# Hybrid MLA and S5 encoder layer: all of x projected ahead of the state tables, and one refinement per latent tile

## The chip, the cores and the metric

The kernel runs on one core of a Trainium2 chip. The metric is the device time of one execution in microseconds; it was measured in three runs, and the median counts. The profile is one execution taken by the hardware profiler.

## What is computed

One inference step of an encoder layer over 1152 tokens of width 1024: 1024 of a new stream, and 8 running streams with 16 new tokens each. One projection of the normalised tokens feeds an attention part (384 numbers of a query latent, 256 of a key and value latent, 32 of a rotary key) and a state space part, S5 (512 channels in 32 groups of 16, each group driving 64 complex states). Behind both come an output projection and a gated feed-forward network with a causal convolution, which is most of the work. Cut to what the change touches (`lb` is the exponential of `a * dt`, `bb` the input matrix scaled by it):

```python
hin = _rmsnorm(x, g_mix_norm) @ w_in
q_lat, c_kv_lat, k_pe, u = split(hin, [384, 256, 32, 512])
c_q  = _rmsnorm(q_lat, g_q_a)              # mean square over 384
c_kv = _rmsnorm(c_kv_lat, g_kv_a)          # mean square over 256, an output
k_pe = _rope(k_pe)                         # an output
s = scan(s[t] = lb * s[t-1] + bb @ u[t])   # per channel group, complex
y = Re(C s) + D * u
o_b = gelu(y) * sigmoid(gelu(y) @ w_glu + b)
h = x + concat(o_a, o_b) @ w_out
out = h + ConvFFN(_rmsnorm(h, g_ffn_norm))
```

`_rmsnorm(v, g)` is `v * rsqrt(mean(v*v) + 1e-6) * g`.

## The kernel before, in words

All matrix products of weight and activation are made of three TensorE passes over a high and a low part of each factor (`mm3`, line 137). The tokens lie in three blocks of 384 columns, block 2 ending with the running streams; a block has three latent tiles of 128 tokens, nine in all (tiles 0 to 8).

Phase A (`phase_a`) is the part around the change. Its pieces:

- `load_x(b, k)` loads a 128-row slice of block b of x (eight make the block), splits it, and sums its squares; `load_w` loads and splits a slice of the projection's weights: `wuh`, `wul` for the S5 channels, `wnh`, `wnl` for the latents.
- `stats(b)` makes the tokens' scale (`ssx`, `rb` on TensorE), and `upart(b)` projects the block to S5 channels: four output blocks `up` of 128x384, 24 matmuls each, scaled to `us` and stored to `u_dram`. With `kouter` it takes the slices in the order in which they come, all four outputs at a time; without, one output after the other.
- `natpart(i)` makes latent tile i: two outputs `nat` (128x384 and 128x288, 24 matmuls each), the Square and the refinement `rsqrt_act` of each (a square root on ScalarE, then a reciprocal and one Newton step on VectorE), and its stores to `cq_dram`, `ckv_dram` and the output.
- `tables()` makes the S5 tables. VectorE and GpSimd form `epre` in 8 pieces, TensorE transposes them (`ep`, four to a piece, line 322), ScalarE evicts to `es` and SyncE stores to `e_dram`; then `fo` in 8 pieces, stored to `f_dram`, and the products `kp` (line 343, four to a piece), evicted to `kts` and stored to `kt_dram`.
- `s5_early` loads `Et` from `e_dram`; `s5_load_u` loads `U` from `u_dram`, in 8 loads of 16 partitions each, in pieces of 144 numbers; both lie in space that the tables' tiles held. `s5_states` multiplies them (`pst`, line 420) and evicts the two parts to `RI`.

Behind that `s5_scan` runs on VectorE and GpSimd (products of complex numbers, lines 373 to 407), and `s5_out` makes the outputs (`py`, line 530) from the states `SP` and a table `Ft`. The sample attention (`b8_q`, `phase_b`: keys `pk`, scores `pS`, rotated keys `pRK`, sums of keys `ssk`) lies beside and behind the scan.

The program is written in one order, but a scheduler orders every engine's list from it, by its own estimates of time; each engine, and SyncE's queue of loads and stores, then works its list strictly in order. Block 1 of x lies in the buffer that block 2 held, so it can be split only when tiles 8, 7 and 6 are done; block 0 has a buffer of its own.

Of the kernel before, what the change touches and what calls it, by code (L numbers as in the profile page):

```python
# [13 lines left out]
AF = mybir.ActivationFunctionType  # L14
# [60 lines left out]
def build(tc, t):  # L75
    nc = tc.nc
# [3 lines left out]
    with root:  # L80
# [69 lines left out]
        def rsqrt_act(pool, y, x, scale, tag):  # L150
            v = pool.tile(list(x.shape), F32, tag=tag + "v", name="rsv")
            w = pool.tile(list(x.shape), F32, tag=tag + "w", name="rsw")
            ts(v, x, scale, EPS, ALU.mult, ALU.add)
            nc.scalar.activation(out=w, in_=x, func=AF.Sqrt, scale=scale, bias=epsc)
            nc.vector.reciprocal(out=y, in_=w)
            stt(w, y, -0.5, y, ALU.mult, ALU.mult)
            mul(w, w, v)
            stt(y, w, 1.5, y, ALU.add, ALU.mult)
# [194 lines left out]
        def s5_early():  # L353
            es = s5t["es"] = root.enter_context(ExitStack())
            s5a = es.enter_context(tc.tile_pool(name="s5a", bufs=1, side="right", reuse_waits="tile"))
            s5t["pool"] = s5a
            Et = s5t["Et"] = s5a.tile([P, G, P], F32, tag="ES", name="Et", padded_shape=[P, G, NCH])
            s5t["U"] = s5a.tile([P, G, NCH], F32, name="U")
            load(Et, e_dram)
# [259 lines left out]
        def phase_a():  # L619
            st = ExitStack()  # L620
            with st:
                a = st.enter_context(tc.tile_pool(name="a", bufs=1))
                sg = st.enter_context(tc.tile_pool(name="asg", bufs=2))
                xb = None
                wnh = a.tile([P, 8, NATW], F32R, name="wnh")
# [3 lines left out]
                def load_x(b, k):  # L629
                    if k == 0:  # L630
                        xp = xb if b == 0 else a
                        xhl[b] = (xp.tile([P, 8, TB], F32R, tag="xhi", name="xhi"),
                                  xp.tile([P, 8, TB], F32R, tag="xlo", name="xlo"))
                    s = al["p"].tile([P, TB], F32, tag="xs", name="xs", bufs=XB[0])
                    load(s, t["xT"][k * P:(k + 1) * P, b * TB:(b + 1) * TB])
                    split(xhl[b][0][:, k], xhl[b][1][:, k], s, gmix[:, k:k + 1])
                    if k == 0:
                        accx[b] = al["p"].tile([P, TB], F32, tag="accx", name="accx", bufs=1)
                        nc.scalar.activation(out=accx[b], in_=s, func=AF.Square)
                    else:  # L640
                        q = al["p"].tile([P, TB], F32, tag="sqx", name="sqx")
                        nc.scalar.activation(out=q, in_=s, func=AF.Square)
                        add(accx[b], accx[b], q, nc.gpsimd if b == 0 else None)

                def load_w(k, hi, lo, c0):
                    n = hi.shape[2]
                    w = al["p"].tile([P, NATW], F32, tag="ws", name="ws", bufs=XB[1])
                    load(w[:, 0:n], t["w_in"][k * P:(k + 1) * P, c0:c0 + n])
                    split(hi[:, k], lo[:, k], w[:, 0:n], eng=nc.gpsimd if k % 2 else None)
# [8 lines left out]
                def stats(b):  # L658
                    c = slice(3 * b, 3 * b + 3)
                    p_ = psum("t", [P, 3], "ssx")  # L660
                    for i in range(3):
                        nc.tensor.matmul(p_[:, i:i + 1], lhsT=accx[b][:, i * P:(i + 1) * P], rhs=ones[:, 0:1], start=True, stop=True)
                    rsqrt_act(al["p"], rx[:, c], p_, 1.0 / DM, "rx")
                    p_ = psum("t", [P, TB], "rb")
                    for i in range(3):
                        rr = al["p"].tile([P, P], F32, tag="rr", name="rr", bufs=3)
                        ts(rr, ones, rx[:, 3 * b + i:3 * b + i + 1], None, ALU.mult)
                        nc.tensor.transpose(p_[:, i * P:(i + 1) * P], rr, ident)
                    Rb[b] = al["p"].tile([P, TB], F32, tag="Rb", name="Rb")
                    acopy(Rb[b], p_)  # L670

                def upart(b, kouter=False):
                    xh, xl = xhl[b]
                    nck = TB // LC
                    pu = {}

                    def step(cb_, k):
                        c0 = cb_ * P
                        if k == 0:
                            pu[cb_] = psum("u", [P, TB], "up")  # L680
                        mm3(pu[cb_], [((wuh[:, k, c0:c0 + P], wul[:, k, c0:c0 + P]), (xh[:, k], xl[:, k]))], first=k == 0, last=k == 7)

                    if kouter:
                        for k in range(8):
                            for cb_ in range(4):
                                step(cb_, k)
                    else:
                        for cb_ in range(4):
                            for k in range(8):
                                step(cb_, k)  # L690
                    for cb_ in range(4):
                        us = al["p"].tile([P, TB], F32, tag="us", name="us").rearrange("p (j c) -> p j c", j=LC)
                        mul(us.rearrange("p j c -> p c j"), pu[cb_].rearrange("p (c j) -> p c j", j=LC),
                            Rb[b].rearrange("p (c j) -> p c j", j=LC))
                        store(u_dram[cb_ * P:(cb_ + 1) * P, :, b * nck:(b + 1) * nck], us)

                def natpart(i):
                    b = i // 3
                    xh, xl = xhl[b]
                    tsl = slice((i % 3) * P, (i % 3 + 1) * P)  # L700
                    n = sg.tile([P, NATW], F32, tag="nat", name="nat")
                    sq = sg.tile([P, 2], F32, tag="sq2", name="sq2")
                    rq = sg.tile([P, 2], F32, tag="rq2", name="rq2")
                    jk = sg.tile([P, QL], BF16, tag="jk2", name="jk2", bufs=1)
                    for z, (c0, c1) in enumerate(((0, QL), (QL, NATW))):
                        p_ = psum("s", [P, c1 - c0], "nat")
                        mm3(p_, [((xh[:, k, tsl], xl[:, k, tsl]), (wnh[:, k, c0:c1], wnl[:, k, c0:c1])) for k in range(8)])
                        acopy(n[:, c0:c1], p_, rx[:, i:i + 1])
                        w = (QL, KL)[z]
                        nc.scalar.activation(out=jk[:, 0:w], in_=n[:, c0:c0 + w], func=AF.Square, accum_out=sq[:, z:z + 1])  # L710
                        rsqrt_act(sg, rq[:, z:z + 1], sq[:, z:z + 1], 1.0 / w, f"rq{z}")
                    cq, ck = n[:, 0:QL], n[:, QL:QL + KL]
                    ts(cq, cq, rq[:, 0:1], None, ALU.mult)
                    store(cq_dram[i * P:(i + 1) * P], cq)
                    stt(ck, ck, rq[:, 1:2], gkv, ALU.mult, ALU.mult)
                    store(ckv_dram[i * P:(i + 1) * P], ck)
                    store(t["ckv"][i * P:(i + 1) * P], ck)
                    x2 = n[:, QL + KL:NATW].rearrange("p (a d) -> p a d", a=2)
                    m1 = sg.tile([P, 2, 16], F32, tag="m1", name="m1")
                    m2 = sg.tile([P, 2, 16], F32, tag="m2", name="m2")  # L720
                    mul(m1, x2, cosb[:, i:i + 1].to_broadcast([P, 2, 16]), nc.gpsimd)
                    mul(m2, x2, sinb[:, i:i + 1].to_broadcast([P, 2, 16]), nc.gpsimd)
                    sub(kpe[:, i, 0:16], m1[:, 0], m2[:, 1], nc.gpsimd)
                    add(kpe[:, i, 16:32], m1[:, 1], m2[:, 0], nc.gpsimd)
# [11 lines left out]
                load(ident, t["ident"])  # L736
                stats(2)
                for k in range(8):
                    load_x(0, k)
                late_consts()  # L740
                load(gkv, t["g_kv"])
                stats(0)
                for k in range(8):
                    load_w(k, wnh, wnl, 0)
                upart(2, True)
                upart(0, True)
                tables()
                s5_early()
                for i in (8, 7, 6):
                    natpart(i)  # L750
                for k in range(8):
                    load_x(1, k)
                stats(1)
                upart(1)
                ust.close()
                s5_open()
                s5_load_u()
                s5_states()
# [966 lines left out]
```

## Time and profile before

| what | us |
|---|---|
| median of the three runs | 1581.94 |
| lowest and highest | 1581.4, 1583.57 |
| span of the profiled execution | 1582.0 |
| TensorE busy | 1497.2 (95%) |
| VectorE busy | 1119.5 (71%) |
| ScalarE busy | 683.8 (43%) |
| GpSimd busy | 320.6 (20%) |

Busy time is the time in which an engine worked on an instruction; what is missing to the span it waited. The page gives the span for the profiled execution and no other time of it. A share over the whole span says little of a stage: the first 400 us hold phase A, the scan and the start of the attention, the other 1180 us the attention's rest and the feed-forward network.

### The profile page before, as it was taken

How to read it: one execution, taken by the hardware profiler on the slowest of the kernel's cores; microseconds unless marked ns; L12 is line 12 of the kernel's file. 1: busy time of each engine (PE TensorE's matmuls, PEld its weight loads, DVE VectorE, ACT ScalarE, POOL GpSimd, SP SyncE). 2: the span in 40 equal slices, each digit the busy share in tenths (PEclk: the TensorE clock that was granted, in tenths of full speed). 3: DMA queues.
4: the chain of work that ended last, by engine and by line, in shares of the span. 5: the costliest groups of instructions: out<-in, count | busy, mean ns of one | idle time of the engine just before them, and what ended most of it. 6: DMA issues, size and time to landing. Idle time of an engine off the chain costs nothing.

```text
span 1582.0 us, 24076 instructions
## 1 busy us (share of the span) xinstructions
PE 1497.2 (95%) x8861; PEld 1427.5 (90%) x8861; DVE 1119.5 (71%) x2376; ACT 683.8 (43%) x1323; POOL 320.6 (20%) x616
## 2 busy tenths in 40 slices
PE   7896857999999999999999999999999999999998
PEld 6876745877888898999999999999999999999998
DVE  8983799485777676367676766776766777777766
ACT  6442346666666676434433333333333333333321
POOL 3550466130444222112100000000100000000000
PEclk9998867999999999999999999999999999999999
DMA  7449343463321222451021111111111111111103
GB/s 203 122 144 161 114 154 57 111 186 97 97 69 48 78 65 65 151 165 52 1 84 37 41 41 41 50 45 40 41 41 41 46 49 51 44 41 40 41 1 130
DMA packets 101205, 122.00 MB, mean 77 GB/s; under 512 B 39240, under 2 KB 81416, under 8 KB 100624
## 3 DMA queue, kind: packets, MB, share of 16 engines
q1 hardware_dynamic: 100960, 120.44, 27.1%
q8 instruction: 69, 1.13, 0.3%
q14 instruction: 48, 0.39, 0.1%
q0 software_dynamic: 128, 0.03, 0.0%
HBM read 93.79 MB, written 26.65 MB: 76 GB/s over the span
## 4 chain that ended last, share of the span: by engine, by line
PE 80%; DVE 11%; DMA 4%; ACT 2%; issue 1%; SPq 1%; POOL 0%; DVEq 0%; ACTq 0%
PE pu L137 35%; PE pd L137 16%; PE pw L137 6%; DVE w L104 3%; PE pk L137 3%; PE pst L1247 2%; PE pg L137 1%; PE pq L137 1%; PE psm L1214 1%; PE pst L1248 1%; PE po L1260 1%; PE po L1262 1%; PE pst L1249 1%; PE pS L137 1%; PE po L1261 1%
## 5 line engine op out<-in xcount | busy, mean ns | idle before, releaser
L104 DVE TENSOR_TENSOR hT<-hT,pd 128x384 f32<-128x384 f32 x528 | 288.2, 551 | 211.7 <-PE pd L137 211.6
L137 PE MATMUL pu<-hnh,wl 128*128 128x384 f32 x1056 | 353.9, 335 | 0.0
L137 PE MATMUL pu<-hnl,wh 128*128 128x384 f32 x1056 | 353.9, 335 | 0.0
L137 PE MATMUL pu<-hnh,wh 128*128 128x384 f32 x1056 | 353.6, 335 | 0.0
L137 PE MATMUL pd<-act,wh 128*128 128x384 f32 x1056 | 348.0, 336 | 0.5 <-DVE hT L104 0.4
L1532 ACT ACTIVATE c<-pu,cvh 128x384 f32<-128x384 f32 x132 | 88.7, 672 | 302.1 <-PE pu L137 302.0
L137 PEld LDWEIGHTS pd<-act,wh 128*128 128x128 f32 x1056 | 197.7, 188 | 2.4 <-DVE hT L104 2.3
L137 PEld LDWEIGHTS pu<-hnh,wh 128*128 128x128 f32 x1056 | 198.2, 188 | 0.0
L137 PEld LDWEIGHTS pu<-hnl,wh 128*128 128x128 f32 x1056 | 198.2, 188 | 0.0
L137 PEld LDWEIGHTS pu<-hnh,wl 128*128 128x128 f32 x1056 | 198.0, 187 | 0.0
L122 DVE SCALAR_TENSOR_TENSOR c<-u,cvh,c 128x256 f32<-128x256 f32 (+1 forms) x352 | 171.1, 516 | 26.8 <-ACT u L101 13.8
L137 PE MATMUL pd<-act,wl 128*128 128x384 f32 x528 | 178.3, 338 | 0.0
L101 ACT ACTIVATE act<-c 128x384 fp32r<-128x384 f32 x66 | 34.7, 526 | 158.8 <-DVE c L104 158.8
L137 PEld LDWEIGHTS pd<-act,wl 128*128 128x128 f32 x528 | 99.2, 188 | 0.0
L1538 POOL COPY u<-u 128x2 f32<-128x2 f32 x88 | 20.0, 228 | 379.1 <-DVE c L104 172.1
L104 DVE TENSOR_TENSOR wl<-ws,wh 128x1024 fp32r<-128x1024 f32 x74 | 91.0, 1234 | 6.0 <-ACT wh L101 6.0
L101 ACT ACTIVATE wh<-ws 128x1024 fp32r<-128x1024 f32 x74 | 78.0, 1057 | 11.7 <-PE pw L137 6.5
L1550 POOL COPY cvo<-u 128x2 f32<-128x2 f32 x44 | 8.1, 184 | 353.9 <-ACT u L101 353.9
L1218 DVE TENSOR_REDUCE mx<-psm 128x1 f32<-128x512 f32 (+2 forms) x96 | 52.3, 550 | 29.8 <-PE psm L1216 15.0
L1554 ACT ACTIVATE c<-c 128x384 f32<-128x384 f32 x66 | 34.7, 526 | 75.1 <-DVE c L122 75.0
L101 ACT ACTIVATE u<-pu 128x384 f32<-128x384 f32 (+2 forms) x176 | 66.2, 404 | 0.0
L137 PE MATMUL pw<-oh,wh 128*128 128x384 f32 x192 | 64.9, 339 | 0.0
(468 smaller groups left out, 3174.6 us busy)
## 6 DMA issues: line engine op xcount, KB each, us to landing
ws<-in_w_up SPq DMA_DIRECT2D x44, 512.0 KB, 3.7
ws<-in_w_down SPq DMA_DIRECT2D x22, 512.0 KB, 3.6
xs<-in_xT SPq DMA_DIRECT2D x24, 192.0 KB, 3.5
os<-o_dram SPq DMA_DIRECT2D x24, 192.0 KB, 2.7
hT<-in_xT SPq DMA_DIRECT2D x24, 192.0 KB, 4.3
out_yT<-hT SPq DMA_DIRECT2D x24, 192.0 KB, 2.1
cf<-in_cT SPq DMA_DIRECT2D x8, 512.0 KB, 4.7
cn<-in_cn SPq DMA_DIRECT2D x8, 512.0 KB, 7.1
```

What stands on the lines that cost most here:

```text
L101: nc.scalar.activation(out=out, in_=in_, func=AF.Copy, scale=scale)
L104: (eng or nc.vector).tensor_tensor(out=out, in0=a, in1=b, op=op)
L122: nc.vector.scalar_tensor_tensor(out=out, in0=a, scalar=s, in1=b, op0=op0, op1=op1)
L137: nc.tensor.matmul(out, lhsT=w, rhs=x, start=first and i == 0, stop=last and i == n - 1)
L1214: nc.tensor.matmul(p_[:, u, 0:n], lhsT=lh, rhs=kT[jj][0][0:QD, 4 * g + h, 0:n], start=True, stop=not dg)
L1218: nc.vector.tensor_reduce(out=mx[:, h, z, hb:hb + 1], in_=p_.rearrange("p a k -> p (a k)")[:, 0:tot], axis=AX.X, op=ALU.max)
L1247: nc.tensor.matmul(o_, lhsT=kh[:, 4 * g + h, ks], rhs=qh[:, h, qs_], start=True, stop=False)
L1248: nc.tensor.matmul(o_, lhsT=kl[:, 4 * g + h, ks], rhs=qh[0:QD, h, qs_], start=False, stop=False)
L1249: nc.tensor.matmul(o_, lhsT=kh[0:QD, 4 * g + h, ks], rhs=ql[:, h, qs_], start=False, stop=not dg)
L1532: nc.scalar.activation(out=c, in_=p_, func=AF.Identity, scale=w[2], bias=w[3])
L1538: nc.gpsimd.tensor_copy(out=u[:, 0:2], in_=halo[i, gv][:, TB:TB + 2])
L1554: nc.scalar.activation(out=g_, in_=g_, func=AF.Silu)
```

## The change

In the program's order, latent weights are loaded ahead of block 0 of x; block 2's channels and its three latent tiles come first; then block 0 and block 1 are loaded and their channels projected, block 1's slice by slice as well; then come the tables and the load of `Et`, and the S5 states. The other six latent tiles stay where they were in the program, behind the S5 states. In `natpart` the Square scales its input, so that its sum is a mean, and one refinement on 128x2 takes the place of two on 128x1.

```diff
--- before.py
+++ after.py
@@ -707,8 +707,8 @@
                         mm3(p_, [((xh[:, k, tsl], xl[:, k, tsl]), (wnh[:, k, c0:c1], wnl[:, k, c0:c1])) for k in range(8)])
                         acopy(n[:, c0:c1], p_, rx[:, i:i + 1])
                         w = (QL, KL)[z]
-                        nc.scalar.activation(out=jk[:, 0:w], in_=n[:, c0:c0 + w], func=AF.Square, accum_out=sq[:, z:z + 1])
-                        rsqrt_act(sg, rq[:, z:z + 1], sq[:, z:z + 1], 1.0 / w, f"rq{z}")
+                        nc.scalar.activation(out=jk[:, 0:w], in_=n[:, c0:c0 + w], func=AF.Square, scale=w ** -0.5, accum_out=sq[:, z:z + 1])
+                    rsqrt_act(sg, rq, sq, 1.0, "rq")
                     cq, ck = n[:, 0:QL], n[:, QL:QL + KL]
                     ts(cq, cq, rq[:, 0:1], None, ALU.mult)
                     store(cq_dram[i * P:(i + 1) * P], cq)
@@ -736,23 +736,23 @@
                 load(ident, t["ident"])
                 stats(2)
                 for k in range(8):
-                    load_x(0, k)
+                    load_w(k, wnh, wnl, 0)
                 late_consts()
                 load(gkv, t["g_kv"])
-                stats(0)
-                for k in range(8):
-                    load_w(k, wnh, wnl, 0)
                 upart(2, True)
-                upart(0, True)
-                tables()
-                s5_early()
                 for i in (8, 7, 6):
                     natpart(i)
                 for k in range(8):
+                    load_x(0, k)
+                stats(0)
+                upart(0, True)
+                for k in range(8):
                     load_x(1, k)
                 stats(1)
-                upart(1)
+                upart(1, True)
                 ust.close()
+                tables()
+                s5_early()
                 s5_open()
                 s5_load_u()
                 s5_states()
```

What the scheduler makes of it: TensorE, at the first table transposes (`ep`). `nat` is a latent tile's output, `up` one of S5 channels. Before:

```order
L137 MATMUL nat<-wnl,xhi 128x384
L137 MATMUL nat<-wnh,xhi 128x384
L322 MATMUL ep<-ident,epre 128x128 [waits DVE_49,PE_49]
L322 MATMUL ep<-ident,epre 128x128 x3
L137 MATMUL nat<-wnh,xlo 128x384
```

Now:

```order
L137 MATMUL up<-xhi,wuh 128x384
L137 MATMUL up<-xhi,wul 128x384
L137 MATMUL up<-xlo,wuh 128x384
L322 MATMUL ep<-ident,epre 128x128 [waits Activation_49]
L322 MATMUL ep<-ident,epre 128x128 x3
L137 MATMUL nat<-wnl,xhi 128x288
```

The first `ep` stood at row 251 of TensorE's list, among latent matmuls; it stands at row 453 now, behind the last projection of block 1, and 288-column latent matmuls follow it.

SyncE's queue, at the loads of `Et` and `U`. Before:

```order
L98 DMA kt_dram<-kts 16x512 [waits DMAHW0_49,DVE_49]
L95 DMA Et<-e_dram 128x32x128 [waits DMAHW1_49,PE_49,Pool_49]
L95 DMA h_1420<-in_h 128x256 [waits DMAHW2_49]
L98 DMA u_dram<-us 1024x1x48 [waits DMAHW3_49,DVE_49]
L98 DMA u_dram<-us 1024x1x48 [waits DMAHW4_49,DVE_49]
L98 DMA cq_dram<-nat 128x384 [waits DMAHW5_49,DVE_49]
L98 DMA u_dram<-us 1024x1x48 [waits DMAHW6_49,DVE_49]
L98 DMA u_dram<-us 1024x1x48 [waits DMAHW7_49,DVE_49]
L98 DMA ckv_dram<-nat 128x256 [waits DMAHW0_49,DVE_49,Activation_49]
L98 DMA out_ckv<-nat 128x256 [waits DMAHW1_49]
L95 DMA U<-u_dram 16x32x144 [waits DMAHW6_49,DMAHW4_49,DMAHW7_49,DMAHW3_49,DMAHW2_49]
L95 DMA U<-u_dram 16x32x144 x2
```

Now:

```order
L98 DMA kt_dram<-kts 16x512 [waits DMAHW3_49,DVE_49]
L95 DMA Et<-e_dram 128x32x128 [waits DMAHW4_49,PE_49,Pool_49]
L95 DMA U<-u_dram 16x32x144 [waits DMAHW6_49,DMAHW5_49,DMAHW3_49]
L95 DMA U<-u_dram 16x32x144
L95 DMA U<-u_dram 16x32x144 [waits DMAHW7_49]
L95 DMA U<-u_dram 16x32x144 [waits DMAHW0_49]
L95 DMA U<-u_dram 16x32x144 [waits DMAHW1_49]
L95 DMA U<-u_dram 16x32x144 [waits DMAHW2_49]
```

Four stores of `u_dram`, three of a latent tile and a load of `h` stood between `Et` and `U`, and the eight loads of `U` now follow `Et` at once.

TensorE, at the S5 states (`pst`). `tq` belongs to the sample attention. Before:

```order
L572 MATMUL tq<-ident,cq_1763 128x128 [waits DMAHW2_49]
L420 MATMUL pst<-U,Et 128x144 [waits DVE_49]
L420 MATMUL pst<-U,Et 128x144 x2
L137 MATMUL nat<-wnl,xhi 128x384
L137 MATMUL nat<-wnh,xhi 128x384
L137 MATMUL nat<-wnh,xlo 128x384
L137 MATMUL nat<-wnl,xhi 128x384
L137 MATMUL nat<-wnh,xhi 128x288
L137 MATMUL nat<-wnh,xlo 128x288
L420 MATMUL pst<-U,Et 128x144 [waits DVE_49]
L137 MATMUL nat<-wnl,xhi 128x288
L420 MATMUL pst<-U,Et 128x144 [waits DVE_49]
```

Now:

```order
L137 MATMUL nat<-wnh,xhi 128x288
L137 MATMUL nat<-wnh,xlo 128x288
L137 MATMUL nat<-wnl,xhi 128x288
L420 MATMUL pst<-U,Et 128x144 [waits DMAHW4_49,DMAHW5_49,DMAHW3_49,DMAHW6_49,DMAHW2_49,DMAHW7_49,DMAHW1_49,DMAHW0_49]
L420 MATMUL pst<-U,Et 128x144 x11
L420 MATMUL pst<-U,Et 128x144 [waits DVE_49]
```

Latent matmuls stood between the `pst` and behind them; now the last latent matmul of the kernel comes directly ahead of the first `pst`, and all 32 `pst` follow one another.

## Rows read from the trace of the kernel before

**Rows 1.** The page: span, busy time of TensorE.

```profile
span 1582.0 us, 24076 instructions
...
PE 1497.2 (95%) x8861; PEld 1427.5 (90%) x8861; DVE 1119.5 (71%) x2376; ACT 683.8 (43%) x1323; POOL 320.6 (20%) x616
```

**Rows 2.** By stage: window, its length, engines' busy us (instructions), clock, DMA share.

```profile
core 0: us, PE busy (x) PEld busy (x) DVE busy (x) ACT busy (x) POOL busy (x), PEclk, DMA share, GB/s
...
117.30:158.30 41.00, 25.89 (x167) 25.55 (x166) 15.85 (x92) 9.26 (x28) 2.79 (x12) 0.85 0.99 157
158.30:174.80 16.50, 16.50 (x108) 16.47 (x109) 8.20 (x20) 8.68 (x22) 0.37 (x1) 0.86 0.82 255
174.80:275.00 100.20, 67.53 (x281) 53.39 (x281) 97.17 (x245) 47.47 (x107) 68.80 (x105) 0.74 0.32 85
275.00:306.00 31.00, 31.00 (x215) 28.84 (x214) 16.08 (x46) 22.06 (x39) 6.31 (x9) 1.00 0.32 85
...
401.60:1582.00 1180.40, 1172.27 (x7110) 1140.83 (x7108) 820.68 (x1602) 480.01 (x914) 165.01 (x413) 1.00 0.19 58
```

**Rows 3.** Timeline, TensorE: start, us, instruction, [idle before, releaser].

```profile
58.38 0.44 PE L137 MATMUL nat<-wnl,xhi 128*128 128x384 f32 x1 [0.64 <-POOL wnl L104]
...
66.44 0.63 PE L322 MATMUL ep<-ident,epre 128*128 128x128 f32 x4 [1.49 <-DVE epre L104]
...
114.91 1.05 PE L343 MATMUL kp<-fo,bb 128*16 128x128 f32 x8
...
158.27 5.49 PE L420 MATMUL pst<-U,Et 128*128 128x144 f32 x24 [15.11 <-DMA krf<-in_kropeT]
...
274.92 0.41 PE L530 MATMUL py<-SP,Ft 128*128 128x144 f32 x2
...
305.91 0.41 PE L530 MATMUL py<-SP,Ft 128*128 128x144 f32 x2
```

**Rows 4.** Timeline, SyncE's queue, from the last table store to U.

```profile
116.85 0.30 SPq L98 DMA_DIRECT2D kt_dram<-kts  x1
117.26 0.60 SPq L95 DMA_DIRECT2D Et<-e_dram  x1
...
135.04 10.12 SPq L95 DMA_DIRECT2D U<-u_dram  x8
```

**Rows 5.** Chain of waits, 110 to 180 us: start, length, what.

```profile
142.67 15.40 DMA U<-u_dram
...
174.80 1.56 DVE w L104 x3
```

**Rows 6.** VectorE's groups up to 265 us: form, count | busy us, mean ns.

```profile
L104 DVE TENSOR_TENSOR rsw<-rsw,rsv 128x1 f32<-128x1 f32 x18 | 6.5, 362 | 0.3
...
L122 DVE SCALAR_TENSOR_TENSOR rsw<-rq 128x1 f32<-128x1 f32 x18 | 6.0, 332 | 0.3
...
L122 DVE SCALAR_TENSOR_TENSOR rq<-rsw,rq 128x1 f32<-128x1 f32 x18 | 4.4, 245 | 0.3
```

**Rows 7.** Timeline, TensorE: two 384-column matmuls in a dense stretch.

```profile
118.05 0.33 PE L137 MATMUL up<-xhi,wul 128*128 128x384 f32 x1
118.22 0.33 PE L137 MATMUL up<-xlo,wuh 128*128 128x384 f32 x1
```

**Rows 8.** By stage, columns as rows 2: table work, dense work, Et, U.

```profile
60.00:120.00 60.00, 51.96 (x314) 45.88 (x313) 53.56 (x116) 22.59 (x53) 38.11 (x36) 0.94 0.47 136
120.00:140.00 20.00, 20.00 (x132) 19.95 (x131) 11.27 (x64) 7.57 (x21) 1.93 (x8) 1.00 0.86 189
118.70:127.00 8.30, 8.30 (x57) 8.26 (x56) 5.58 (x38) 2.18 (x6) 0.00 (x0) 1.00 0.99 272
136.00:157.00 21.00, 7.16 (x47) 6.84 (x45) 3.30 (x15) 2.90 (x10) 0.87 (x4) 0.74 1.20 120
```

## The prediction, made before the changed kernel was run

> **What bounds the kernel now.** I read the page first: TensorE is busy for 1497.2 of 1582.0 us, so the end is set by TensorE wherever nothing holds it up [rows 1]. Then the span cut into stages, to see where it is held up. From 401.6 us on it is busy for 1172.27 of 1180.40 us at full clock; nothing there is touched, and that stretch can only start earlier or later. The stages ahead are where a change can act: 117.3 to 158.3 (25.89 busy of 41.00), and 174.8 to 275, where VectorE is busy for 97.17 of 100.20 and TensorE for 67.53 [rows 2].
>
> Then the timeline and the chain, to see what hands the stages on. The first transpose of the state tables (`ep`) starts at 66.44, the last product (`kp`) at 114.91 [rows 3]; SyncE, one queue in order, issues the last `kt_dram` store at 116.85 and the load of Et behind it at 117.26, and the loads of U only from 135.04 [rows 4], since the last `u_dram` stores (block 1) come out late. TensorE then stands idle for 15.11 us until `pst` starts at 158.27 [rows 3]. That row names another load as the releaser; the chain says what it waited for: U [rows 5]. Behind `pst` the S5 scan starts on VectorE (174.80), and the output products `py` run from 274.92 to 305.91 [rows 3, 5]. So to first order the path is: table end, Et and U, `pst`, scan on VectorE, `py`, then a TensorE queue with hardly a gap. It gives the price rule: a microsecond on the path ahead of the scan is a microsecond at the end, except for TensorE work that leaves the stretch behind the scan.
>
> A run here varies by some 2 us (1581.4 to 1583.57), so 0.2%, 3.2 us, is what can be told from no change. The profiled span of 1582.0 is the median of the runs (1581.94) within 0.1 us, and the sum is made against it.
>
> **Part 1: one refinement per tile.** Per tile one Sqrt on ScalarE and five VectorE operations of 128x1 go, 9 and 45 in all; the Square's scale replaces a multiply that the refinement did. The rows give, for 18 each, 6.5 + 6.0 + 4.4 us [rows 6]; half of them is 8.5 us, and the two short ones (reciprocal, scale and add) bring it to some 10 us of VectorE. In 117.3 to 158.3 VectorE is busy for 15.85 of 41 us [rows 2], so most of it lies where VectorE waits anyway, and I give it nothing there. In the scan stage the changed order has no latent tile left at all, which frees more, but it has also pulled sample attention (sums of keys, their refinements) in there: counted from instructions by their rows, VectorE's list from the first scan operation to the second final state goes from 94.5 to 97.7 us. That is +3, not a gain.
>
> **Part 2: where the tables end.** The changed TensorE order puts 114 projections of S5 channels and 72 + 50 latent matmuls ahead of the first `ep`, counted from 58.4 us, up to which the two orders do the same. Dense pitch of a 384-column matmul is 0.17 us [rows 7]; a 288-column one has three quarters of that, 0.13. So 186 x 0.172 + 50 x 0.131 = 38.5, and 1.5 for the small ones: first `ep` at 99, not 66.4. Behind it, up to the last `kp`, stand 32 transposes, 66 + 70 latent matmuls and 32 `kp`: a group of four `ep` takes 0.63 us and one of four `kp` (eight passes) 1.05 [rows 3], so 5.0 + 20.5 + 8.4 = 34. Dense, the last `kp` is at 133.5. But in 60 to 120, the same kind of mix, TensorE was busy for 51.96 of 60 us (87%), against 20.00 of 20 in 120 to 140 where no table work runs [rows 8]. With 87% in both pieces it is at 145. I take 140: the first piece has little table work between its matmuls and should run nearly dense, and the second is loaded with transfers (by the queue's list some 10 MB between 104 and 142 us, 260 GB/s, where 60 to 120 moved 136). Et is then issued 2.35 us behind, as before (114.91 to 117.26): **142, 24.5 later than before**.
>
> The cover lost: in the kernel before, 24 projections and five latent tiles stood behind the tables and filled the wait for Et and U. Now three tiles are left to fill it, 54 x 0.172 + 72 x 0.131 = 18.7 us, and the rest of a wait of some 32 us is idle.
>
> **Part 3: Et and U.** SyncE now issues U right behind Et; every `u_dram` store is long done. Before, 17.8 us lay between the two issues. Et's packets took 8.3 us at 272 GB/s, U's 21.0 at 120, both with the DMA engines full (share 0.99 and 1.20) [rows 8], so I put them one behind the other: 1.4 to the first packet, 8.4, 20.9, and 1.4 to the matmul, 32 in all. `pst` starts at 174, 15.7 later. Not lower than 24 (U wholly beside Et), not higher than 41 (the span from Et to `pst` before); I take 32 since full engines have no room for both.
>
> The Trainium skill ("DMA: Bandwidth & Descriptors", Specifications) lets transfers run at line rate from 512 bytes on; U's rows are 576 bytes. By that U would move like Et, and the sum would end 12 us lower. The trace disagrees: 120 GB/s against 272.
>
> **Part 4: pst, scan, outputs.** Before, latent matmuls stood among the `pst`, and the scan started 16.5 us behind the first of them [rows 2]. Of the 108 passes of that stretch 64 are `pst`'s; the other 44, at some 0.14 us, are 6 us that now lie elsewhere, which leaves 10.5. (The first 24 took 5.49 [rows 3], so the evictions between must keep up; between 10 and 14.) Scan start 184.5, +9.7. The scan takes 97.7 x 100.2 / 94.5, that is 103: its second final state comes at 287.5, +12.5. Behind it TensorE before did 31.0 us of dense work up to the last `py`, of which the new order has done 24 `pk`, 12 weight products and 12 score products ahead, inside the scan where TensorE is idle for a third of the time [rows 2]. That leaves some 20 us there, and 0.9 more than before behind it. Net: +12.5 - 11 + 0.9 = +2.4; plus one stall of GpSimd of about 1 us in its part of the scan (its order now has cache conversions between the scan's steps). **+3.5: 1585.5 us.** This case by itself: table end 140 to 145, 1583 to 1590.
>
> **Rivals.**
> **TensorE runs dense through the tables.** For it: the work of VectorE for the tables is done while the projections run, so fewer `ep` should wait. Last `kp` 134, Et at 136: 6 us less, 1579.5, which can't be told from no change; under Et at 138 the change starts to win.
> **U runs beside Et.** U's slow rate may be one of its queue, not of the engines. For it: 120 GB/s is under half of what the same engines moved shortly before. Against it: they count as full. `pst` 8.4 earlier: 1577.
> **U at Et's rate** (the page's rule above). 2.36 MB at 272 GB/s is 8.7 us, not 20.9: 1573. Only if what slowed U before was something else in flight.
> **Transfers are late, and the tables with them.** The changed queue holds sample caches, weights and latent stores ahead of the last `kt_dram` stores and of Et. If one of them waits, or the 10 MB make the `es` and `kts` buffers come free late, Et is issued at 150: 8 us more, 1593. It decides from an Et issue past 145.
> **Nothing comes of the order change** is excluded: the instruction lists differ as the program does.
>
> **How the numbers follow.** Chances: forecast 0.38 (0.10 within 0.2%, 0.28 above); TensorE dense 0.22 (0.14 within, 0.08 faster); U beside Et 0.16 (faster); U at Et's rate 0.06 (faster); late transfers 0.12 (slower); 0.06 for others, an even third each. Together faster 0.32, within 0.2% 0.26, slower 0.42. The range takes in late transfers at the top (1594) and reaches down to U beside Et with some of the dense gain (1574); the page's rule is left out.
>
> **What would show it.** In the changed profile: first `ep` at 97 to 103, last `kp` at 137 to 145, Et's issue 2 to 3 us behind it, U's issues right behind Et's, `pst` idle for 10 us or more and starting some 32 us after Et's issue, scan start 10 to 11 us after that, scan 100 to 105 us, last `py` 18 to 22 us after its end. I am wrong if `pst` starts before 165, if the scan stage is no longer bound by VectorE (below 90% busy), or if the difference at the end is not within 3 us of that at the last `py`.

## The result, and the profile after

The changed kernel takes 1594.52 us (median of four runs, 1593.45 to 1595.72), the kernel before 1582.76 in the runs beside it (1581.4 to 1583.63): a ratio of 1.0074, 95% interval 1.0059 to 1.0088. It is slower, by some 11.8 us. The forecast was slower by 3.5, to 1585.5, with a range of 1574 to 1594: the side was right, the size a third of what came, and the time lies half a microsecond above the range. The profiled execution has a span of 1592.0, 2.5 below the median, and is compared with the span of 1582.0 [rows 1].

The page of the changed kernel, span and busy time:

```profile
span 1592.0 us, 24024 instructions
...
PE 1497.7 (94%) x8861; PEld 1426.4 (90%) x8861; DVE 1107.5 (70%) x2331; ACT 679.4 (43%) x1312; POOL 320.6 (20%) x616
```

TensorE has the same work (1497.7 us against 1497.2), VectorE 12 us less: the 45 operations are gone, and with them 1% of its time. Nearly all of the 10.0 us between the two profiles is TensorE's idle time, 94.3 us against 84.8. The table by stage of the changed kernel, cut at the first `ep`, the end of the last `kp`, the first `pst`, the start of the scan, its end, the last `py`, and 95.7 us behind it ([rows 2] has the same cuts from the first `pst` on):

```profile
core 0: us, PE busy (x) PEld busy (x) DVE busy (x) ACT busy (x) POOL busy (x), PEclk, DMA share, GB/s
58.40:97.50 39.10, 39.10 (x238) 38.80 (x237) 27.80 (x69) 13.79 (x36) 16.54 (x23) 1.00 0.32 88
97.50:135.60 38.10, 35.41 (x234) 30.70 (x232) 30.99 (x54) 14.59 (x35) 25.00 (x25) 0.96 0.76 216
135.60:176.30 40.70, 20.00 (x131) 19.38 (x131) 8.22 (x59) 6.40 (x19) 1.79 (x8) 0.80 1.04 182
176.30:188.00 11.70, 11.66 (x69) 10.97 (x70) 7.18 (x18) 8.38 (x22) 1.28 (x5) 0.81 0.14 35
188.00:287.00 99.00, 58.66 (x212) 42.88 (x211) 96.94 (x238) 44.94 (x95) 69.37 (x97) 0.69 0.34 81
287.00:311.90 24.90, 24.90 (x177) 23.08 (x177) 8.30 (x23) 14.97 (x26) 2.92 (x4) 1.00 0.43 106
311.90:407.60 95.70, 85.12 (x450) 72.90 (x449) 57.26 (x127) 61.16 (x103) 16.79 (x21) 0.96 0.49 136
407.60:1592.00 1184.40, 1175.28 (x7113) 1142.61 (x7111) 820.44 (x1603) 480.08 (x913) 163.92 (x413) 1.00 0.19 58
```

Up to the first `ep` TensorE runs without a gap at full clock, as the sum had it, and nearly so through the tables (35.41 of 38.10). Then half of 40.70 us is idle: three latent tiles, then the wait for U. In the scan TensorE is idle for 40.3 us, 7.7 more than before, and does 212 passes where it did 281. Behind the last `py` it is idle for 10.6 and 9.1 us; the kernel before has 8.1 in its last row [rows 2] and 7.7 in the second row here, ahead of it:

```profile
58.40:174.80 116.40, 93.25 (x580) 86.80 (x581) 76.98 (x214) 41.37 (x103) 41.27 (x49) 0.90 0.70 159
306.00:401.60 95.60, 87.88 (x447) 75.01 (x446) 58.41 (x127) 59.55 (x102) 16.73 (x21) 0.95 0.51 141
```

The first row here says that from 58.4 us to the start of the scan TensorE idled for 23.2 us before, and in the changed kernel it idles for 23.4 (the first four rows of the table above). So the idle time did not grow ahead of the scan, though the delay arose there: TensorE did 13 us more work ahead of the scan, and that work is missing inside it, where VectorE sets the length.

Five rows of TensorE's timeline answer to [rows 3], one of VectorE's (in a fence of its own) to [rows 5]:

```profile
97.51 0.49 PE L322 MATMUL ep<-ident,epre 128*128 128x128 f32 x3
...
134.53 1.05 PE L343 MATMUL kp<-fo,bb 128*16 128x128 f32 x8
...
176.34 5.90 PE L420 MATMUL pst<-U,Et 128*128 128x144 f32 x29 [19.96 <-DMA out_ckv<-nat]
...
291.67 0.41 PE L530 MATMUL py<-SP,Ft 128*128 128x144 f32 x2
...
311.68 0.41 PE L530 MATMUL py<-SP,Ft 128*128 128x144 f32 x2
```

```profile
187.97 0.47 DVE L104 TENSOR_TENSOR w<-RI,SG 128x176 f32<-128x176 f32 x1
```

And SyncE's queue, against [rows 4]:

```profile
137.54 0.32 SPq L98 DMA_DIRECT2D kt_dram<-kts  x1
...
144.00 0.31 SPq L98 DMA_DIRECT2D kt_dram<-kts  x1
144.42 0.59 SPq L95 DMA_DIRECT2D Et<-e_dram  x1
145.74 18.63 SPq L95 DMA_DIRECT2D U<-u_dram  x8
```

The first `pst` waits 19.96 us. The row names a store; by TensorE's list (see "The change") it waits for all eight loads of U, and I take those for the cause, as in [rows 3, 5]. Step by step, forecast and measured:

| step | before | forecast | measured |
|---|---|---|---|
| first `ep` | 66.4 | 99 | 97.5 |
| last `kp` begins | 114.9 | 140 | 134.5 |
| Et issued | 117.3 | 142 | 144.4 |
| first `pst` | 158.3 | 174 | 176.3 |
| scan starts | 174.8 | 184.5 | 188.0 |
| scan ends | 274.9 | 287.5 | 287 |
| last `py` | 305.9 | 308 | 311.7 |
| end | 1582.0 | 1585.5 | 1592.0 |

### The profile page after: what moved, and what is told of

It reads as the page before. It is cut to its first block, busy times and chain, and to the rows that moved or that the text cites. A ratio compares the mean times of both kernels' runs of the same rounds, so it can differ in the third digit from the quotient of the medians.

```text
span 1592.0 us, 24024 instructions
## 1 busy us (share of the span) xinstructions
PE 1497.7 (94%) x8861; PEld 1426.4 (90%) x8861; DVE 1107.5 (70%) x2331; ACT 679.4 (43%) x1312; POOL 320.6 (20%) x616
## 4 chain that ended last, share of the span: by engine, by line
PE 77%; DVE 8%; ACT 1%; SPq 1%; DMA 1%; issue 0%; POOL 0%; ACTq 0%; DVEq 0%
PE pu L137 35%; PE pd L137 16%; PE pw L137 6%; DVE w L104 2%; PE pst L1247 2%; PE pk L137 2%; PE pg L137 2%; PE pq L137 1%; PE psm L1214 1%; PE pst L1248 1%; PE po L1260 1%; PE po L1262 1%; PE pst L1249 1%; PE po L1261 1%; PE pZ L1013 1%; DVE hT L104 1%
## 5 line engine op out<-in xcount | busy, mean ns | idle before, releaser
L137 PEld LDWEIGHTS pd<-act,wl 128*128 128x128 f32 x528 | 99.1, 188 | 0.0
```

The source lines that it names most:

```text
L137: nc.tensor.matmul(out, lhsT=w, rhs=x, start=first and i == 0, stop=last and i == n - 1)
```

## The experiments

Theory P: the loss is the path's. The table end came 27 us later, Et, U, the `pst` and the scan behind it, and the end follows the start of the scan. Theory F: the loss is made in and behind the scan, since no latent matmul is left to fill TensorE there. Theory R: the shared refinement costs.

The kernel before was run again beside each group of runs, and each ratio is taken against those. It took 1582.59 us beside the first four runs, 1583.42 beside the fifth to the eighth, 1584.0 beside the ninth to the twelfth and 1583.87 beside the thirteenth and fourteenth; its 27 executions beside the first four span 1578.28 to 1586.39. So a difference of a few microseconds between two single executions, as between two profiles, says little.

### Order alone, refinement alone

The first run has the changed order and the refinement of before, the second the reverse. Edit of the first (the second makes the opposite edit in the kernel before):

```diff
-nc.scalar.activation(out=jk[:, 0:w], ..., scale=w ** -0.5, accum_out=sq[:, z:z + 1])
-rsqrt_act(sg, rq, sq, 1.0, "rq")
+nc.scalar.activation(out=jk[:, 0:w], ..., accum_out=sq[:, z:z + 1])
+rsqrt_act(sg, rq[:, z:z + 1], sq[:, z:z + 1], 1.0 / w, f"rq{z}")
```

> The changed order with the old refinement (two per latent tile). Theory P (the loss is the order's: the table end moved from 117 to 144 us, and Et, U, the S5 states and the scan with it): the loss stays or grows by what the 45 VectorE operations are worth, 1593 to 1600 us, Et issued at 143 to 148. Theory R (the joint refinement itself costs, since the query half of a tile now waits for the other half's Square): the loss shrinks by more than half, below 1588.

> The order of before with the shared refinement alone. Theory P: VectorE waits in most of that stretch, so between nothing and 4 us faster than before, 1578 to 1583. Theory R: slower than before, 1586 or more.

Order alone: 1593.94 us, ratio 1.0067 (1.0054 to 1.0081); Et issued at 145.3. Refinement alone: 1582.32, ratio 0.9995 (0.9986 to 1.0004). The loss is the order's, within these intervals all of it; theory R falls. The 45 operations are worth nothing that can be measured, as the sum had it.

### Block 1 behind the tables again

The edit, with several statements put on one line:

```diff
-for k in range(8): load_x(1, k)
-stats(1); upart(1, True); ust.close()
 tables()
 s5_early()
+for k in range(8): load_x(1, k)
+stats(1); upart(1, True); ust.close()
 s5_open()
```

> The change, but block 1 of x loaded and projected behind the tables, as before. Theory P: the table end goes back to 120 to 130 us, and U, now late by its own stores, is issued at 140 to 150; S5 states at 163 to 172, and the time is between the two kernels, 1583 to 1590. Theory F (the loss is made in and behind the scan, since no latent matmul is left to fill TensorE there, and not by the table end): still 1591 or more, as the latent tiles lie ahead of the S5 states here too.

1582.72 us, ratio 0.9998 (0.9987 to 1.0008): the whole loss is gone, though latent weights, tiles 8, 7 and 6 and the other tiles stand as in the change. Et is issued at 122.0, U at 146.0, the scan starts at 180.4:

```profile
180.36 0.46 DVE L104 TENSOR_TENSOR w<-RI,SG 128x176 f32<-128x176 f32 x1
```

So block 1's projection ahead of the tables is the part that costs. Theory F expected 1591 or more and falls. Theory P expected 1583 to 1590, and the time came out just below: the scan starts 7.6 us earlier than in the changed kernel, but the end comes 11.8 earlier. By the profiles the last `py` stands 118.1 us behind the start of the scan here and 123.7 in the changed kernel, so the start of the scan does not carry the whole gain.

### U and Et in a place of their own

The weights of the S5 channels move to a pool on the other side, and U and Et take their space when block 1 is projected, so that U needn't wait for the tables' space; the eighth run also has four buffers for `kts`. The edit, cut to its main lines:

```diff
-au = ust.enter_context(tc.tile_pool(name="au", bufs=1))
-wuh = au.tile([P, 8, SW], F32R, name="wuh")
+au = s5t["pool"] = es.enter_context(tc.tile_pool(name="s5a", side="right", ...))
+wuh = au.tile([P, 8, SW], F32R, tag="U", name="wuh", padded_shape=[P, 8, SW + 64])
...
+s5_load_u()
 tables()
 s5_early()
 s5_open()
-s5_load_u()
```

> The change with U and Et placed where the S5 channels' weights lie, so that U is loaded as soon as block 1's channels are stored and not behind Et. Theory P: the first S5 state starts about 11 us behind Et's issue and not 32, the scan some 18 us earlier, and the end 12 to 18 us earlier than the changed kernel: 1577 to 1583. Theory F: the scan starts earlier by as much, but the end by less than 6 us: above 1588.

> U and Et in the place of the S5 channels' weights, as in the fourth run, and four buffers for kts. The eviction of the S5 states there waited for the tables' last store (157.9 us), whose space it takes. Theory P: the tables' last store comes 6 to 12 us earlier, the scan starts at 162 to 170 and not 172.6, and the end is 3 to 9 us before that run: 1571 to 1577, faster than both kernels. Theory F: within 2 us of that run.

1579.93 us, ratio 0.9994 (0.998 to 1.0008), and 1581.89, 0.9993 (0.9982 to 1.0004). In the fourth run U is issued at 105.2, beside the tables, the first `pst` starts at 151.7 and the scan at 172.6, 15.3 us earlier than in the changed kernel; the end is 14.6 earlier:

```profile
105.24 10.17 SPq L95 DMA_DIRECT2D U<-u_dram  x8
```

```profile
172.63 0.47 DVE L104 TENSOR_TENSOR w<-RI,SG 128x176 f32<-128x176 f32 x1
```

Theory P again: the end moves with the start of the scan. The buffers of the eighth run brought the scan to 169.8, and nothing at the end, where 3 to 9 us were expected: a miss. Its profile shows where the gain went: the first `py` from the states `SP` starts 5.2 us earlier than in the fourth run (273.3, 278.5), but the last 1.0 later (300.0, 299.0), since TensorE does 188 passes between them and not 157.

### What holds Et behind the last product

From the start of the last `kp` row to the issue of Et there are 9.9 us in the changed kernel (134.53 to 144.42), 2.35 before. ScalarE waited for a store of `kts` to land, and SyncE for loads, by the waits of SyncE in 135 to 146 us:

```profile
SPq L95 <- DMA wk<-in_w_k: 3.3, 1, 3.3
SPq L98 <- DMA wq<-in_w_q: 2.2, 1, 2.2
SPq L95 <- DMA wkT<-in_w_kT: 0.8, 1, 0.8
```

The fifth run takes the buffers' wait away (`kts`, six buffers in place of two), the thirteenth the loads, the fourteenth both. Edit of the thirteenth, with the like for `wkT`:

```diff
+for x_ in (wq[:, 0, 0:1], wk[:, 0, 0:1]):
+    nc.gpsimd.tensor_copy(out=x_, in_=s5t["Et"][:, 0, 0:1])
 load(cq, cq_dram[i8 * P:])
 load(wq, t["w_q"].rearrange("(k p) n -> p k n", p=P))
```

> The changed kernel with six buffers in place of two for the evicted products of the second table (kts). In the changed trace the last product is formed at 135.3 but Et is issued only at 144.4, VectorE having waited 10.4 us for stores of that tile to land. Theory P: Et is issued 4 to 8 us earlier (136 to 140), the first S5 state and the scan start as much earlier, and the end by 3 to 8 us: 1587 to 1591. Theory F (the end is made in and behind the scan): Et as early, but the end within 2 us of the changed kernel, 1592.5 to 1596.

> The changed kernel with the sample attention's three weight loads (2.2 MB) held until Et has landed, by one tiny write into each tile; in the changed kernel they stand in SyncE's queue ahead of the last two table stores and of Et. Theory D (Et comes 9 us behind the last table product because these loads fill the engines and SyncE's queue): Et is issued at 136 to 140 and not 144.4, and scan start and end come 4 to 8 us earlier: 1586 to 1590. Rival (the tables' own chain sets it): Et within 2 us of 144.4 and the end at 1592 to 1597. If Et is early and the end is not, the sample attention's weights have become the wait.

> As the run before, with six buffers for kts. Theory D: with the queue free the buffers are a limit of their own, and Et comes 1 to 4 us earlier than in that run. If Et is the same, they never were.

Buffers alone: 1596.96 us, ratio 1.0087 (1.0067 to 1.0108), Et at 146.1; neither theory's figure, since Et did not come earlier. (The wait of 10.4 us that its expectation gives to VectorE is ScalarE's in the trace.) The evictions no longer wait there, and the last of them is done by 135.5, but its store is still issued only at 145.2, behind waits for the same three loads:

```profile
L104 DVE TENSOR_TENSOR kts<-kts,dd x8: 205/214/1176, 124.2 to 135.2; 16x64 f32<-16x64 f32 x8
L98 SPq DMA_DIRECT2D kt_dram<-kts x8: 309/324/860, 125.4 to 145.2; - x8
```

Loads held back: 1582.83, ratio 0.9995 (0.9985 to 1.0005), 11.7 us below the changed kernel. Its queue at the same place:

```profile
136.41 0.33 SPq L98 DMA_DIRECT2D kt_dram<-kts  x1
...
138.64 0.30 SPq L98 DMA_DIRECT2D kt_dram<-kts  x1
139.35 0.60 SPq L95 DMA_DIRECT2D Et<-e_dram  x1
140.21 18.72 SPq L95 DMA_DIRECT2D U<-u_dram  x8
```

The last `kp` row begins at 136.7 there, and Et follows 2.7 us behind, much as before the change. So it was the three loads: they stand ahead of the last table stores in SyncE's queue, and later entries wait for them to land. (Whether their traffic also slowed other transfers, these runs don't tell apart.) Both edits: 1580.31 in one run, Et at 138.7, 0.7 earlier than with the loads alone, where 1 to 4 were expected. The scan starts 5.3 us earlier with the loads held (182.6), as expected, but the end comes 11.5 earlier by the profiles, where 4 to 8 were expected. The rest lies in what TensorE does inside the scan. By stage, the scan and the `py` of the thirteenth run:

```profile
182.60:286.80 104.20, 69.16 (x280) 52.22 (x279) 102.75 (x252) 51.59 (x106) 71.28 (x101) 0.72 0.31 83
286.80:300.90 14.10, 14.10 (x110) 13.84 (x109) 2.39 (x10) 6.16 (x13) 0.00 (x0) 1.00 0.58 146
```

The scan ends when it did (286.8), but TensorE did 280 passes in it and not 212, and the `py` stage is 14.1 us and not 24.9. TensorE had come through its list there: the first `py` from the states `SP` starts 3.1 us ahead of the scan's end, and waits for `SP`; in the changed kernel it starts 4.7 us behind it, without a wait.

```profile
283.66 0.51 PE L530 MATMUL py<-SP,Ft 128*128 128x144 f32 x2 [1.15 <-ACT SP L101]
```

The sample attention's first wait (19.3 us for `ex`) is the same in both, and TensorE's waits for ScalarE's squares (`sq`) fall from 5.9 us to 1.3. Why they do stays open.

### U's rate

The prediction took U's 120 GB/s as the rate of full DMA engines, and weighed the length of its rows beside it. The next runs vary the shape of the load in the changed kernel. The sixth, seventh and fifteenth read the same bytes of `u_dram` in another order (U then holds the numbers in other places, so that the S5 outputs are of other numbers): eight loads of 16 partitions or one of 128, rows of 18 KB or of 576 bytes.

```diff
-for j in range(LC):
-    load(s5t["U"][GS * j:GS * j + GS], u_dram.rearrange("(g c) j k -> j c g k", c=GS)[j])
+load(s5t["U"], u_dram.rearrange("s j k -> (s j k)").rearrange("(p g k) -> p g k", p=P, g=G))
```

This is the seventh; the sixth keeps the loop over 16 partitions, and the fifteenth reads `(g p k)`.

> The changed kernel with U read as if u_dram were laid out the way U lies: the same bytes, the same eight loads of 16 partitions, but in rows of 18 KB and not of 576 bytes. It changes the computation: U holds u_dram's numbers in another order, so the S5 outputs are of other numbers. If U's slow rate comes from its short rows, its packets take 9 to 12 us and not 21, the first S5 state starts some 10 us earlier (164 to 168) and the end 7 to 11 us earlier, 1583 to 1588. If it comes from 16 partitions per load, or from moving beside and behind Et, nothing changes: 1592 to 1596.

> As the run before, with one load over 128 partitions in place of eight of 16; U again holds u_dram's numbers in another order. If 16 partitions per load set the rate, this one is the faster of the two, with U's packets in 8 to 9 us; if the short rows did, both are alike.

> As the seventh run (the changed kernel, one load of U over 128 partitions), but in rows of 576 bytes, 32 to a partition; U again holds u_dram's numbers in another order, so the S5 outputs are of other numbers. The ninth to twelfth run did not have the 576-byte rows that their expectation names: with the channels in the new order a partition's row is one piece of 18 KB. If the number of partitions per load alone set U's rate, U's packets take 6 to 9 us here too and the first S5 state starts at 160 to 166. If short rows matter once all partitions take part, U takes 10 us or more.

The stretch in which U's packets run, by stage (columns as above; the last two are what to read): first the changed kernel, then the sixth, the fifteenth and the seventh run.

```profile
156.00:174.00 18.00, 0.38 (x3) 0.15 (x2) 0.00 (x0) 0.00 (x0) 0.00 (x0) 0.62 1.22 124
```

```profile
158.00:172.00 14.00, 0.81 (x7) 0.58 (x5) 0.00 (x0) 0.00 (x0) 0.00 (x0) 0.68 0.97 135
```

```profile
155.00:162.00 7.00, 2.49 (x19) 2.26 (x17) 0.00 (x0) 0.00 (x0) 0.00 (x0) 0.98 1.14 299
```

```profile
155.00:160.00 5.00, 3.68 (x27) 3.45 (x25) 0.43 (x2) 0.00 (x0) 0.00 (x0) 1.00 1.01 424
```

| | rows of 576 bytes | rows of 18 KB |
|---|---|---|
| eight loads of 16 partitions | 124 GB/s | 135 |
| one load of 128 partitions | 299 | 424 |

Going from eight loads of 16 partitions to one of 128 makes most of the difference, and the rows come second. No run has one load of 16 partitions or several of 128, so the partitions per load and the number of loads are not told apart. That SyncE takes long to issue eight loads is not the reason: in the kernel before all eight are issued by 145.2 [rows 4], and U's packets run on to 157 at 120 GB/s [rows 8]. The DMA engines count as busy (0.97 to 1.22) in all four. The time follows: 1591.45 us for the sixth (ratio 1.0054, 1.0035 to 1.0072), 1582.05 in one run of the fifteenth (the kernel before took 1579.44 in one run beside it), 1577.66 in one run of the seventh.

The other four runs fill U with its own numbers by one load: the S5 channels are projected in another order (channel within the group first), and `u_dram` is laid out like U.

```diff
-u_dram = dram.tile([SW, LC, NCH], F32, name="u_dram")
+u_dram = dram.tile([LC, GS * G, NCH], F32, name="u_dram")
...
+if n == SW:
+    v = [x.rearrange("p (c g) -> p c g", c=GS) for x in v[:2]] + [v[2].rearrange("p (g c) -> p c g", c=GS)]
...
-store(u_dram[cb_ * P:(cb_ + 1) * P, :, b * nck:(b + 1) * nck], us)
+store(u_dram[:, cb_ * P:(cb_ + 1) * P, b * nck:(b + 1) * nck].rearrange("j q k -> q j k"), us)
...
-for j in range(LC):
-    load(s5t["U"][GS * j:GS * j + GS], u_dram.rearrange("(g c) j k -> j c g k", c=GS)[j])
+load(s5t["U"], u_dram.rearrange("j (c g) k -> (j c) g k", c=GS))
```

> The changed kernel with the S5 channels held in another order (channel within the group first), so that U is read by one load over all 128 partitions, in rows of 576 bytes as before; the outputs are unchanged. The seventh run read the same bytes by one load over 128 partitions in rows of 18 KB. If the number of partitions per load sets U's rate, the first S5 state starts 10 to 16 us earlier than in the changed kernel (160 to 166) and the end falls to 1574 to 1583. If the short rows matter as well, half of that: 1585 to 1589.

> The kernel before with the same one load of U. Theory P (the path runs over U into the scan): U is issued at about 135 as before, its packets take 7 to 12 us in place of 21, the scan starts 9 to 14 us earlier and the end is 6 to 14 us earlier: 1568 to 1577, faster than both kernels. Theory F (the end is made in and behind the scan): 1579 to 1583.

> The third run's order (block 1 behind the tables) with the one load of U. Theory P: as the run before, within 4 us of it, 1568 to 1578.

> The eighth run (U and Et in a place of their own, four buffers for kts) with the one load of U. There U had landed long before Et, so its rate is not on the path: within 3 us of that run, 1579 to 1585. If it falls by more, U's slow load was costing something else, such as the stores behind it in SyncE's queue.

The first of these expectations misdescribes its kernel: in the new layout a partition's row is one piece of 18 KB. The results, beside 1584.0 us of the kernel before: the changed kernel with one load 1581.74, ratio 0.9983 (0.9971 to 0.9995); **the kernel before with one load 1566.20, ratio 0.9892 (0.9875 to 0.991), faster than both kernels** and than the 1568 to 1577 expected; the third run's order 1574.22, 0.9946 (0.9926 to 0.9967), inside its 1568 to 1578 but 8.0 us above the kernel before with one load, where 4 were expected at most; the eighth run's places 1569.37, 0.9913 (0.9897 to 0.9928). TensorE's timeline and SyncE's queue of the best:

```profile
144.11 2.08 PE L419 MATMUL pst<-U,Et 128*128 128x144 f32 x15
```

```profile
117.08 0.63 SPq L95 DMA_DIRECT2D Et<-e_dram  x1
135.14 0.32 SPq L95 DMA_DIRECT2D U<-u_dram  x1
```

U is issued when it was before (135.0), and the first `pst` starts 9.0 us behind it, not 23.2. With one load the change costs 15.5 us (1581.74 against 1566.20), more than with eight: the first `pst` stand 20.6 us apart (164.7 and 144.1), with eight 18.1.

The twelfth run fell by 12.5 us against the eighth where at most 3 were expected. In the eighth the issues of U take 10 us of SyncE's queue, ahead of table stores; with one load, Et is issued at 132.6 and not 139.0, and the scan starts at 161.5 and not 169.8. That accounts for 8.3 of the 12.5; the expectation named this as the other possibility, and no run tests it by itself.

## Why the prediction was right and where it was wrong

The end follows the start of the scan. First scan operation and span of the profiled executions, and their difference:

| kernel | scan starts | span | difference |
|---|---|---|---|
| before | 174.8 | 1582.0 | 1407.2 |
| changed | 188.0 | 1592.0 | 1404.0 |
| order alone | 184.6 | 1591.6 | 1407.0 |
| refinement alone | 177.4 | 1578.4 | 1401.0 |
| block 1 behind | 180.4 | 1578.8 | 1398.4 |
| U early | 172.6 | 1578.3 | 1405.7 |
| U early, four `kts` | 169.8 | 1579.6 | 1409.8 |
| six `kts` | 191.1 | 1595.9 | 1404.8 |
| loads held | 182.6 | 1580.5 | 1397.9 |
| one load, changed | 176.8 | 1581.6 | 1404.8 |
| one load, before | 161.9 | 1566.6 | 1404.7 |
| one load, U early, four `kts` | 161.5 | 1566.3 | 1404.8 |

The other five profiles lie between 1397.8 and 1404.5. The scan's start moves over 30 us, and what lies behind it over 12, which is one execution each and in part what TensorE still has to do when the scan ends. So the price rule with which the prediction began stands to first order, and it was right that the table end would be late, that U would come straight behind Et, and that the refinement would bring nothing.

**What failed is the size, and the step that failed is the payback behind the scan.** By the profiles the end came 6.5 us later than forecast, 1592.0 and not 1585.5 (the changed kernel's median lies another 2.5 above its profile). Up to the end of the scan the sum came out: 287.0, with 287.5 forecast. Behind it 10.1 us were to come back, 11 in the `py` stage less 0.9 behind it, and 2.1 did. That is 8.0 us too little; the 0.5 at the scan's end, and 1 us forecast for a stall of GpSimd that cost nothing, bring it down to the 6.5.

The step "of which the new order has done 24 `pk`, 12 weight products and 12 score products ahead, inside the scan where TensorE is idle for a third of the time" took what stands ahead in the list for done. At the end of the scan TensorE was 4.7 us behind in its list (22 passes, the `py` only from 291.7). From the first `py` to the last it then took the 20 us of the forecast, so the stage fell from 31.0 us to 24.7 and not to 20, and 6.3 us came back where 11 were forecast. The other part lies behind the last `py`: 1280.3 us were left there where 1276.1 were before, 4.2 more and not 0.9. That part is not explained, and with one execution each it can't be told from the spread of the executions: over all 17 profiles it lies between 1275.7 and 1283.1. It is one of the signs of being wrong that the prediction had named, since the difference at the end (10.0) is not within 3 us of that at the last `py` (5.8).

That the scan ended on time is luck, since two errors cancel: it started 3.5 us late (188.0, 184.5 forecast) and was 4 shorter (99.0, 103 forecast). The start first. "Et is then issued 2.35 us behind, as before" was wrong: TensorE ran denser than I took it (last `kp` at 134.5, which is the first rival's 134), and Et came 9.9 us behind it. Again two errors nearly cancel, to 144.4 against 142. The rival "Transfers are late, and the tables with them" named the mechanism, sample caches and weights in the queue ahead of the last table stores, and gave it 0.12; its sign, an issue past 145, was just missed, and the thirteenth run shows it at work. A part of it belonged in the forecast: the list of SyncE's queue was there to be read. The other microsecond is the `pst`, 11.7 us and not 10.5.

The scan was too long in the forecast because 100.2 us, which the sum stretched by VectorE's count, were GpSimd's. The operations that make the final states, first in the kernel before, then in the changed one:

```profile
L104 DVE TENSOR_TENSOR fin<-w,RI x2: 251/271/291, 267.3 to 270.8; 128x88 f32<-128x88 f32 x2
L104 POOL TENSOR_TENSOR fin<-w,RI x2: 269/298/326, 273.7 to 274.9; 128x40 f32<-128x40 f32 x2
```

```profile
L104 POOL TENSOR_TENSOR fin<-w,RI x2: 267/269/271, 281.2 to 283.7; 128x40 f32<-128x40 f32 x2
L104 DVE TENSOR_TENSOR fin<-w,RI x2: 248/250/251, 285.4 to 286.8; 128x88 f32<-128x88 f32 x2
```

Before, GpSimd's second final state came 4 us behind VectorE's, and now it comes 3 us ahead of it. Up to VectorE's own second final state the scan went from 96.2 us to 99.1, which is the 3 us that the count had. So GpSimd, whose stall was put at 1 us, did not lengthen the scan. Three sums of the prediction are also rounded off a little: the first `ep` comes to 98.4 and not 99, the last `kp` at 87% to 144 and not 145, the scan to 103.6 and not 103. None of them changes this account.

Part 3 came out on time (31.9 us from Et's issue to the first `pst`, 32 forecast), and its reason was wrong. "Full engines have no room for both" read the share as a capacity: U moves 124 GB/s with the engines at 1.22, and 299 at 1.14 when one load spans all partitions. The rule weighed there, line rate from 512 bytes on (the Trainium skill, "DMA: Bandwidth & Descriptors", Specifications), is not borne out either. At 16 partitions longer rows change little, so the rows were not what mainly held U back; at 128 they bring 299 to 424 GB/s, so rows of 576 bytes stay below the full rate there. Another page bears on it: the Trainium skill ("SBUF — State Buffer", section "Door 1: The DMA port swizzle (why `[64,N]` ≈ `[32,N]`)") says that a transfer's rate goes by how many of 16 ports its partitions reach, and gives 104 GB/s for partitions 0 to 15 at 1 MiB. The trace agrees in kind: 124 and 135 GB/s for loads of 16 partitions, 299 and 424 for one of 128.

## What to carry to other kernels

Find the one start that the end follows (here the scan's) and price a reordering by what it does to that start; work moved ahead of it to fill a wait pays nothing if it delays what is waited for. What stands ahead in an in-order list is done only if the engine gets there: count the work left behind a stage from where the engine will be, not from the list. And before a slow transfer is taken for a limit, look at how many partitions one load spans: the busy share of the DMA engines was the same, near 1, from 124 to 424 GB/s, and is no measure of how much more they could move.

## What the runs showed of the hardware

Eight loads over 16 partitions each moved 124 GB/s in rows of 576 bytes and 135 in rows of 18 KB; one load of the same bytes over 128 partitions moved 299 and 424. The DMA engines were shown as busy at 0.97 to 1.22 in all four. Of SyncE's queue: an entry can wait for an earlier load to land that is for another tile. SyncE waited 6.3 us for three weight loads (2.2 MB) ahead of the last 32 KB table store and of Et, and with these loads held back Et was issued 5.1 us earlier.
